# A Strassen-like product for one more K tile pair of the MLP's second matrix, with its blocks in another order

## The chip, the cores and the metric

The kernel runs on one NeuronCore of a Trainium2 chip. Five engines matter here: TensorE (PE in the profile, and PEld for its weight loads), VectorE (DVE), ScalarE (ACT), GpSimd (POOL, nearly unused here) and SyncE (SP, which issues nearly all of the DMA transfers). Matrices lie in the on-chip memory with 128 partitions; results of TensorE go to PSUM, which has 8 banks of 128 x 512 float32, and are carried off by DVE and ACT. The metric is the device time of one execution in microseconds (us).

## The reference

The reference is a trunk of two decoder layers over 256 positions of width 2048, in float32. What it computes, cut to its core:

```python
for layer in range(2):
    mix = short_conv_mixer(h, ...) if layer == 0 else mla_mixer(h, ...)   # conv, then attention
    h = layer_norm(ALPHA * h + mix, ...)
    h = layer_norm(ALPHA * h + sq_relu_mlp(h, w1[layer], w2[layer]), ...)

def sq_relu_mlp(x, w1, w2):        # x 256 x 2048, w1 2048 x 8192, w2 8192 x 2048
    return jnp.square(jax.nn.relu(x @ w1)) @ w2
```

The change touches the MLP of both layers, and the first load of the kernel.

## The kernel before

Every float32 matrix is used as two parts, a high part (a cast to a reduced float32 format that TensorE multiplies at full pace) and a low part (what the cast left out). ACT makes the high part (L122), DVE the low part (L123); the helper is `split`. A product then takes three passes of TensorE, high by high, high by low and low by high. In `dot` (L284 to L286) each of the three is one matmul of 512 columns. In `products` (W1) the low part of the activations lies beside the high part, so the three passes are one matmul of 512 columns (`high`, L200) and one of 256 (`low`, L204): a pair per K tile.

The weights come through one ordered list, `stream`. Its items are taken in that order by `take`, which on the way loads and splits items that lie ahead, up to `LOOK` = 5 units. A plain item is 128 x 1024 numbers (512 KB), one load on SP, one split, one unit. A fast item is two loads, and counts three units: `prepare` (L143 to L166) makes from its two arrays the seven right-hand factors of a Strassen-like product, with three splits of 1024 columns, one of 512 (`t4`) and three subtractions on DVE (L155, L158, L161). Split parts lie in `whl` (8 buffers each for high and low), loaded arrays in `raws` (5 buffers). The program order is that of the Python text; each engine's own queue is ordered by a planner of the framework, which may move work that is ready ahead of work that is not.

The MLP (`mlp`, L565) works through the 8192 hidden features in eight quarters q of 1024 features ("quarter" is this document's word; there are eight of them, `NQ`). In each, W1 makes eight tiles of 128 hidden features (`products`, eight tiles of 16 pairs; q = 0 goes another way, L661 to L679), and `hidden` carries each tile off: ACT copies half of the PSUM tile, DVE adds the halves (L341), ACT takes relu and square, two tiles at a time are split into `h`, and `form` makes the left-hand factors S1 to S4 of the fast product. Then W2 takes the quarter's eight K tiles into the output of 256 x 2048, which is held in `acc` as two token halves t by four blocks n of 512 columns.

In the quarters `FAST` (q = 1 to 6), blocks 0 and 1 go by `first_pair` (L601): for each of the four pairs j of K tiles, the 2 x 2 block product (two token halves by two K tiles by two column blocks) is done with seven products in place of eight (`fast_products`, L328), into seven PSUM banks. Three of the seven sums are carried into `acc`, the four others into `sums` (`keep`, L593 to L599); `fold` (L610) adds those into `acc` in six DVE instructions during q = 7. Blocks 2 and 3 follow as plain products (`down`, L296): per block, four items of two K tiles, each item with two token halves, two K tiles and three matmuls. The W1 tiles of the quarters use PSUM banks 0 and 1 in turn (L682). In layer 2 the residual is turned by TensorE transposes in the quarters 1 to 4, between block 2 and block 3 (`extra`, `turn_residual`, L953).

At the start, the first four K tiles come each as one array of 768 columns, 256 of the input and 512 of weights (`lead`, L512 to L516). The second of them is issued by ACT, the others by SP.

Of the kernel before, what the change touches and what calls it, by code (L numbers as in the profile page):

```python
# [10 lines left out]
F32 = mybir.dt.float32  # L11
# [5 lines left out]
P = 128  # L17
W = 256 + 2
T = 256
D = 2048  # L20
NC = D // P
FF = 4 * D
NQ = 8
# [11 lines left out]
NB = 4  # L35
BW = D // NB
FAST = range(1, NQ - 1)
FIRST = (0, 1, 2, 3, 4, 6, 8, 12, 16)
LEAD = 4
HEAD = 4  # L40
# [11 lines left out]
def trunk(ctx: ExitStack, tc: tile.TileContext, xT, vecs, lead, w_first, w_in, w_out, w_kv, w_q, w_uk, w_uv,  # L52
# [28 lines left out]
    def mlp_stream(l):  # L81
        out = []
        for q in range(NQ):
            out += halves(w1[l, q * QC:(q + 1) * QC])
            plain = halves(w2[l, q, 2:] if q in FAST else w2[l, q])
            fast = [(w2f[l, q, j, 0], w2f[l, q, j, 1]) for j in range(QC // 2)] if q in FAST else []
            at = 0 if q or q not in FAST else len(plain) // 2
            out += plain[:at] + fast + plain[at:]
        return out

    stream += mlp_stream(0) + halves(w_kv) + halves(w_q)
# [181 lines left out]
    def products(n, x, turned=None, banks=(None,)):  # L273

        for i in range(n):
            w = take()
            ps = psum("ps_u", banks[i % len(banks)])
            mm_run([(w, ps)], x, 0, NC, NC, turned=None if i else turned)
            yield ps


    def dot(ps, w, x, first, last):

        nc.tensor.matmul(ps, x[0], w[0], start=first, stop=False)  # L284
# [37 lines left out]
    OWN, KEPT = ("1", "5", "7", "6"), (2, 3, 4, 5, 6, 7, 0)  # L322
# [5 lines left out]
    def fast_products(ps, x, forms, j, n):  # L328

        b, = take(1)  # L330
        a = {"11": held(x[2 * j], 0), "12": held(x[2 * j + 1], 0), "22": held(x[2 * j + 1], 1)}
        for i in range(4):
            a[f"S{i + 1}"] = [forms[:, j, o, i * P:(i + 1) * P] for o in range(2)]
        for p, l, r in FACTORS:
            dot(ps[p], b[r], a[l], j == 0, j == n - 1)

    def whole(ps, out):

# [173 lines left out]
    for k0, k1 in pieces:  # L512
        if k0 < LEAD:
            r = raws.tile([P, 1024], F32, tag="raw", name=f"lead{k0}")
            (nc.sync if k0 != 1 else nc.scalar).dma_start(r[:, :T + HEAD * P], lead[k0])
# [49 lines left out]
    def mlp(idx, ln, blocks, fast, begin=None, extra=None):  # L565
# [14 lines left out]
        def block(n, t):  # L580
            return acc[:, t, n * BW:(n + 1) * BW]
# [11 lines left out]
        def keep(p, ps):  # L593

            at = sums[:, OWN.index(p)] if p in OWN else block(*{"2": (0, 0), "3": (1, 0), "4": (0, 1)}[p])
            if q == 0 or q == FAST[0] and p in OWN:
                nc.scalar.copy(at, ps)
            else:
                nc.vector.tensor_tensor(at, at, ps, ALU.add)  # L599

        def first_pair(h, forms, banks):  # L601

            n = QC // 2
            ps = {p: psum(f"ps_f{p}", bank) for (p, _, _), bank in zip(FACTORS, banks)}
            for j in range(n):
                fast_products(ps, h, forms, j, n)
            for p in ps:
                keep(p, ps[p])

        def fold():  # L610

            s1, s5, s7, s6 = (sums[:, i] for i in range(4))
            both = acc[:, 1, :2 * BW].rearrange("p (b c) -> p b c", b=2)
            right = acc[:, :, BW:2 * BW]
            two = lambda v: v.unsqueeze(1).to_broadcast([P, 2, BW])
            for d, a, b in ((block(0, 0), block(0, 0), s1), (s6, s6, s1), (block(1, 0), block(1, 0), s6),
                            (s7, s7, s6), (both, both, two(s7)), (right, right, two(s5))):
                nc.vector.tensor_tensor(d, a, b, ALU.add)
                yield

        for q in range(NQ):
            ht = act.tile([P, QC, 2 * T], F32R, tag="c", name=f"h{idx}_{q}")
            h = [ht[:, k, :] for k in range(QC)]
# [80 lines left out]

# [409 lines left out]
```

## Time and profile before

| | us |
|---|---|
| median of 3 runs | 2025.61 (2025.37 to 2025.71) |
| the profiled execution | 2025.47 |
| its span, first to last instruction | 2023.7 |
| PE busy / PEld busy | 2016.2 / 1762.2 |
| DVE busy / ACT busy | 1606.0 / 1175.8 |
| HBM read | 381.78 MB, 190 GB/s over the span |
| one quarter q = 2 (540.22 to 625.45) | 85.23 |
| of it W1, blocks 0 and 1, blocks 2 and 3 | 44.39, 19.08, 21.76 |

The profile's group rows read: line of the kernel, engine, operation, tiles written and read, shape and count, busy time and mean duration of one, idle time of the engine before it and what ended that. The mean of a matmul is longer than the step from one matmul to the next, because matmuls are pipelined; steps are read from start times, or from a stretch and a count. In the answers by stretch, each engine's column is its busy time and, in brackets, its instructions.

### The profile page before, as it was taken

Reading aid. Unit: us, or ns where it says so; the run is one execution under the profiler, and the core shown is the slowest. Engines: PE = TensorE matmul, PEld = TensorE weight load, DVE = VectorE, ACT = ScalarE, POOL = GpSimd, SP = SyncE. Lnnn points to the kernel's source line nnn. Section 1 sums busy time; section 2 is a strip of 40 time slices with the busy share of each in tenths; the row PEclk is TensorE's granted clock in tenths of the full one; section 3 lists DMA queues with packets and bytes.
Section 4 is the critical chain, followed back from the end, with each engine's and each line's share of the span. In section 5 each row is a group of like instructions: output and inputs, shape, how many; then the busy total and the mean of one; then the engine's idle time right before and its main releaser. Section 6 shows DMA issues by size and latency. Waiting matters only on the chain.

```text
span 2023.7 us, 30065 instructions
## 1 busy us (share of the span) xinstructions
PE 2016.2 (100%) x11240; PEld 1762.2 (87%) x11240; DVE 1606.0 (79%) x2472; ACT 1175.8 (58%) x1802; POOL 2.3 (0%) x21
## 2 busy tenths in 40 slices
PE   9999999999999999999999999999999999999998
PEld 8888888988888888888889998898888888888886
DVE  7667677788797987879688978776879798797966
ACT  6444445676565665656556655567656556565651
POOL 0000000000000000000000000000000000000000
PEclk9999999999999999999999999999999999999999
DMA  9666666564756657466754544656475664746663
GB/s 320 203 188 189 189 189 186 174 197 140 255 152 214 210 165 248 146 231 200 216 176 151 181 129 136 191 177 197 137 246 168 203 224 144 248 155 211 220 203 119
DMA packets 106705, 385.83 MB, mean 191 GB/s; under 512 B 11840, under 2 KB 12480, under 8 KB 106304
## 3 DMA queue, kind: packets, MB, share of 16 engines
q1 hardware_dynamic: 106416, 383.53, 60.5%
q8 instruction: 88, 1.44, 0.3%
q14 instruction: 57, 0.47, 0.1%
q10 hardware_dynamic: 144, 0.39, 0.1%
HBM read 381.78 MB, written 2.10 MB: 190 GB/s over the span
## 4 chain that ended last, share of the span: by engine, by line
PE 99%; DMA 0%; DVE 0%; ACT 0%; issue 0%; DVEq 0%
PE ps_u L200 20%; PE ps_l L200 13%; PE ps_u L204 11%; PE ps_d L284 7%; PE ps_d L286 7%; PE ps_d L285 7%; PE ps_l L204 7%; PE ps_f L285 4%; PE ps_f L286 4%; PE ps_f L284 4%; PE ps_w L234 2%; PE ps_w L232 2%; PE ps_w L233 2%; PE ps_g L232 1%; PE ps_g L234 1%; PE ps_g L233 1%
## 5 line engine op out<-in xcount | busy, mean ns | idle before, releaser
L123 DVE TENSOR_TENSOR lo<-raw,hi 128x1024 fp32r<-128x1024 f32 x710 | 860.2, 1222 | 314.3 <-ACT hi L122 243.3
L122 ACT CAST hi<-raw 128x1024 fp32r<-128x1024 f32 x710 | 742.3, 1050 | 461.9 <-PE ps_u L200 105.6
L200 PE MATMUL ps_u<-xhl,hi 128*128 128x512 f32 x1792 | 621.0, 392 | 0.0
L204 PE MATMUL ps_u<-xhl,lo 128*128 128x256 f32 x1792 | 499.7, 280 | 0.0
L200 PEld LDWEIGHTS ps_u<-xhl,hi 128*128 128x128 f32 x1792 | 334.5, 187 | 72.1
L204 PEld LDWEIGHTS ps_u<-xhl,lo 128*128 128x128 f32 x1792 | 339.2, 189 | 1.8
L284 PE MATMUL ps_d<-hi,h 128*128 128x512 f32 x640 | 250.0, 391 | 0.0
L286 PE MATMUL ps_d<-hi,h 128*128 128x512 f32 x640 | 249.3, 390 | 0.0
L285 PE MATMUL ps_d<-lo,h 128*128 128x512 f32 x640 | 249.2, 389 | 0.0
L200 PE MATMUL ps_l<-xhl_a,hi 128*128 128x512 f32 x704 | 243.5, 393 | 0.0
L204 PE MATMUL ps_l<-xhl_a,lo 128*128 128x256 f32 x704 | 195.1, 279 | 0.0
L200 PEld LDWEIGHTS ps_l<-xhl_a,hi 128*128 128x128 f32 x704 | 131.9, 188 | 29.4
L286 PEld LDWEIGHTS ps_d<-hi,h 128*128 128x128 f32 x640 | 120.2, 188 | 25.0
L284 PEld LDWEIGHTS ps_d<-hi,h 128*128 128x128 f32 x640 | 120.2, 188 | 24.8 <-DVE fh L341 0.3
L285 PEld LDWEIGHTS ps_d<-lo,h 128*128 128x128 f32 x640 | 120.2, 188 | 24.7
L204 PEld LDWEIGHTS ps_l<-xhl_a,lo 128*128 128x128 f32 x704 | 132.3, 189 | 0.2
L200 PE MATMUL ps_l<-z,hi 128*128 128x512 f32 x240 | 83.9, 399 | 0.0
L652 ACT ACTIVATE fp<-fp 128x256 f32<-128x256 f32 x96 | 40.0, 417 | 74.5 <-DVE fp L341 73.7
L122 ACT CAST hi_t<-raw_t 128x1024 fp32r<-128x1024 f32 x48 | 50.4, 1049 | 41.7 <-DVE raw_t L155 33.4
L234 PE MATMUL ps_w<-xd,hi 128*128 128x258 f32 x256 | 73.0, 285 | 0.0
L232 PE MATMUL ps_w<-xd,hi 128*128 128x258 f32 x256 | 72.6, 284 | 0.0
L233 PE MATMUL ps_w<-xd,lo 128*128 128x258 f32 x256 | 72.5, 283 | 0.0
(261 smaller groups left out, 3134.1 us busy)
## 6 DMA issues: line engine op xcount, KB each, us to landing
raw<-in_w_dram SPq DMA_DIRECT2D x416, 512.0 KB, 4.4
raw<-in_w2f_dram SPq DMA_DIRECT2D x96, 512.0 KB, 3.7
raw<-in_w_in_dram SPq DMA_DIRECT2D x88, 512.0 KB, 3.7
raw<-in_w_out_dram SPq DMA_DIRECT2D x32, 512.0 KB, 3.6
raw<-in_w_o_dram SPq DMA_DIRECT2D x32, 512.0 KB, 3.9
raw<-in_w_kv_dram SPq DMA_DIRECT2D x10, 512.0 KB, 4.3
raw<-in_w_q_dram SPq DMA_DIRECT2D x8, 512.0 KB, 4.4
raw<-in_w_uk_dram SPq DMA_DIRECT2D x8, 512.0 KB, 4.5
```

Of the source, the lines that this page charges most:

```text
L122: nc.scalar.copy(hi, src)
L123: nc.vector.tensor_tensor(lo, src, hi.bitcast(F32), ALU.subtract)
L200: nc.tensor.matmul(ps, w[blk // 8][0][:, blk % 8, :], x, start=first, stop=False)
L204: nc.tensor.matmul(ps[:, :T], w[blk // 8][1][:, blk % 8, :], x[:, :T], start=False, stop=last)
L232: nc.tensor.matmul(ps[:, :W], hi, x[k][:, :W], start=k == 0, stop=False)
L233: nc.tensor.matmul(ps[:, :W], lo, x[k][:, :W], start=False, stop=False)
L234: nc.tensor.matmul(ps[:, :W], hi, x[k][:, W:], start=False, stop=k == NC - 1)
L284: nc.tensor.matmul(ps, x[0], w[0], start=first, stop=False)
L285: nc.tensor.matmul(ps, x[0], w[1], start=False, stop=False)
L286: nc.tensor.matmul(ps, x[1], w[0], start=False, stop=last)
L652: nc.scalar.activation(f, f, AF.Relu)
```

## The change

- **Order of blocks.** In the quarters 1 to 6, blocks 2 and 3 come first and blocks 0 and 1 after them. `down_pairs` replaces `first_pair` and the two calls of `down`, and goes pair by pair over the K tiles.
- **One more fast pair.** `MIXED = "pspp"`: of the four pairs of K tiles of blocks 2 and 3, the second ("s") goes by the seven products too. Products 2, 3 and 4 of it, and the part "22", add into the same four PSUM banks as the plain products of the other pairs; the other four (`OWN`) have banks of their own and are carried into `sums` right after, which is twice as large now. Each quarter thus ends with 15 adds out of PSUM in place of 11, and `fold` has eight instructions of 1024 columns.
- **One matmul in two.** `EVEN`: in the last K tile of one bank, the second of the three matmuls of `dot` is issued as two of 256 columns each, so that a quarter's W2 has an even number of matmuls.
- **Banks.** W1's tiles use four PSUM banks in turn; which four rotates from quarter to quarter (`busy`, `free`). The transposes of `extra` come before the last pair of K tiles.
- **Order of arrays.** The large arrays are laid out in another order and without the small gaps between them; the scratch kept for DMA descriptors shrinks from 4096 to 512 bytes per partition.
- **First K tile.** Its input part is issued by ACT and its weight part by SP; the second K tile moves to SP.

```diff
+MIXED = "pspp"
+EVEN = (QC - 1, "22")
...
-    for tag, columns in (("c", 4096), ("pad0", 64), ("b", 8256), ("a1", 4128), ("pad1", 96), ("a2", 4128), ("pad2", 96)):
+    for tag, columns in (("c", 4096), ("a2", 4128), ("a1", 4128), ("b", 8256)):
...
-            plain = halves(w2[l, q, 2:] if q in FAST else w2[l, q])
-            fast = [(w2f[l, q, j, 0], w2f[l, q, j, 1]) for j in range(QC // 2)] if q in FAST else []
...
+            for j, kind in enumerate(MIXED):
+                out += [(w2f[l, q, 1, j, 0], w2f[l, q, 1, j, 1])] if kind == "s" else \
+                    halves(w2[l, q, 3, j]) + halves(w2[l, q, 2, j])
+            out += [(w2f[l, q, 0, j, 0], w2f[l, q, 0, j, 1]) for j in range(QC // 2)]
...
-    def dot(ps, w, x, first, last):
+    def dot(ps, w, x, first, last, two=False):
         nc.tensor.matmul(ps, x[0], w[0], start=first, stop=False)
-        nc.tensor.matmul(ps, x[0], w[1], start=False, stop=False)
+        for at in (slice(0, T), slice(T, 2 * T)) if two else (slice(None),):
+            nc.tensor.matmul(ps[:, at], x[0], w[1][:, at], start=False, stop=False)
         nc.tensor.matmul(ps, x[1], w[0], start=False, stop=last)
...
-            (nc.sync if k0 != 1 else nc.scalar).dma_start(r[:, :T + HEAD * P], lead[k0])
+            for queue, at in ((nc.scalar, slice(0, T)), (nc.sync, slice(T, T + HEAD * P))) if k0 == 0 else \
+                    ((nc.sync, slice(0, T + HEAD * P)),):
+                queue.dma_start(r[:, at], lead[k0][:, at])
...
-        sums = fast.tile([P, 4, BW], F32, name=f"sums{idx}")
+        sums = fast.tile([P, 4, 2, BW], F32, name=f"sums{idx}")
...
+        def down_pairs(h, forms, busy, free):
+            ps = {p: psum("ps_d", bank) for p, bank in zip(("22", "3", "2", "4"), free)}
+            for j, kind in enumerate(MIXED):
+                if kind == "s":
+                    first, last = j == MIXED.index("s"), j == MIXED.rindex("s")
+                    if first:
+                        ps.update({p: psum(f"ps_f{p}", bank) for p, bank in zip(OWN, busy)})
+                    fast_products(ps, h, forms, j, OWN if first else (), OWN if last else ())
+                    if last:
+                        for p in OWN:
+                            keep(p, 1, ps[p])
+                    continue
+                if extra and q <= NB and j == len(MIXED) - 1:
+                    for t in range(2):
+                        extra(block, q - 1, t, busy[2 + t])
+                for nb, two in ((3, ((1, "22"), (0, "3"))), (2, ((0, "2"), (1, "4")))):
+                    w, = take(1)
+                    for t, p in two:
+                        for kk in range(2):
+                            k = 2 * j + kk
+                            dot(ps[p], wide_rows(w, kk), held(h[k], t), k == 0, k == QC - 1, (k, p) == EVEN)
+                    if j == len(MIXED) - 1:
+                        for _, p in two:
+                            keep(p, 1, ps[p])
             n = QC // 2
+            banks = (*busy, *free)
             ps = {p: psum(f"ps_f{p}", bank) for (p, _, _), bank in zip(FACTORS, banks)}
             for j in range(n):
-                fast_products(ps, h, forms, j, n)
+                fast_products(ps, h, forms, j, ps if j == 0 else (), ps if j == n - 1 else ())
             for p in ps:
-                keep(p, ps[p])
+                keep(p, 0, ps[p])
+            return (banks[7], *banks[:3]), banks[3:7]
...
+        busy, free = (0, 1, 2, 3), (4, 5, 6, 7)
...
-                for m, ps in enumerate(products(QC, xhl, TURNED, (0, 1))):
+                for m, ps in enumerate(products(QC, xhl, TURNED, busy)):
...
-                first_pair(h, forms, KEPT)
-                for n, banks in ((2, (1, 2)), (3, (3, 4))):
-                    down(h, put, n, banks)
-                    if extra and n == 2 and q <= NB:
-                        for t in range(2):
-                            extra(block, q - 1, t, 5 + t)
+                busy, free = down_pairs(h, forms, busy, free)
...
-    nc = _bacc.Bacc("TRN2", target_bir_lowering=False, num_devices=1, dynamic_dma_scratch_size=4096)
+    nc = _bacc.Bacc("TRN2", target_bir_lowering=False, num_devices=1, dynamic_dma_scratch_size=512)
```

More of the change, by code (lines that the diff above doesn't have):

```diff
@@ L84, in mlp_stream @@
             out += halves(w1[l, q * QC:(q + 1) * QC])
-            plain = halves(w2[l, q, 2:] if q in FAST else w2[l, q])
-            fast = [(w2f[l, q, j, 0], w2f[l, q, j, 1]) for j in range(QC // 2)] if q in FAST else []
-            at = 0 if q or q not in FAST else len(plain) // 2
-            out += plain[:at] + fast + plain[at:]
+            if q not in FAST:
+                out += halves(w2[l, q])
+                continue
[3 more added lines that the diff above has]
+            out += [(w2f[l, q, 0, j, 0], w2f[l, q, 0, j, 1]) for j in range(QC // 2)]
         return out
@@ L320, in down_late, with fast_products @@
                 put(n, t, ps)
-    OWN, KEPT = ("1", "5", "7", "6"), (2, 3, 4, 5, 6, 7, 0)
+    OWN = ("1", "5", "7", "6")
     FACTORS = (("3", "S4", "22"), ("1", "11", "11"), ("5", "S1", "T1"), ("7", "S3", "T3"),
                ("2", "12", "21"), ("6", "S2", "T2"), ("4", "22", "T4"))
-    def fast_products(ps, x, forms, j, n):
+    def fast_products(ps, x, forms, j, fresh, ready):
         b, = take(1)
@@ L334, in fast_products @@
         for p, l, r in FACTORS:
-            dot(ps[p], b[r], a[l], j == 0, j == n - 1)
+            dot(ps[p], b[r], a[l], p in fresh, p in ready)
     def whole(ps, out):
@@ L589, in put, with keep @@
                 nc.vector.tensor_tensor(block(n, t), block(n, t), ps, ALU.add)
-        sums = fast.tile([P, 4, BW], F32, name=f"sums{idx}")
-        def keep(p, ps):
-            at = sums[:, OWN.index(p)] if p in OWN else block(*{"2": (0, 0), "3": (1, 0), "4": (0, 1)}[p])
-            if q == 0 or q == FAST[0] and p in OWN:
+        sums = fast.tile([P, 4, 2, BW], F32, name=f"sums{idx}")
+        def keep(p, g, ps):
+            at = sums[:, OWN.index(p), g, :] if p in OWN else \
+                block(*{"2": (2 * g, 0), "3": (2 * g + 1, 0), "4": (2 * g, 1), "22": (2 * g + 1, 1)}[p])
+            if q == FAST[0] and p in OWN:
                 nc.scalar.copy(at, ps)
@@ L599, in keep @@
                 nc.vector.tensor_tensor(at, at, ps, ALU.add)
-        def first_pair(h, forms, banks):
+        def down_pairs(h, forms, busy, free):
[9 more added lines that the diff above has]
+                            keep(p, 1, ps[p])
+                    continue
+                if extra and q <= NB and j == len(MIXED) - 1:
[10 more added lines that the diff above has]
+                            keep(p, 1, ps[p])
@@ L603, in first_pair @@
             n = QC // 2
+            banks = (*busy, *free)
             ps = {p: psum(f"ps_f{p}", bank) for (p, _, _), bank in zip(FACTORS, banks)}
             for j in range(n):
-                fast_products(ps, h, forms, j, n)
+                fast_products(ps, h, forms, j, ps if j == 0 else (), ps if j == n - 1 else ())
             for p in ps:
-                keep(p, ps[p])
+                keep(p, 0, ps[p])
+            return (banks[7], *banks[:3]), banks[3:7]
         def fold():
             s1, s5, s7, s6 = (sums[:, i] for i in range(4))
-            both = acc[:, 1, :2 * BW].rearrange("p (b c) -> p b c", b=2)
@@ L614, in fold @@
[L614 to L617, printed above, removed]
+            c = acc.rearrange("p t (g b c) -> p t b g c", g=2, b=2)
+            for d, a, b in ((c[:, 0, 0], c[:, 0, 0], s1), (s6, s6, s1), (c[:, 0, 1], c[:, 0, 1], s6), (s7, s7, s6),
+                            (c[:, 1, 0], c[:, 1, 0], s7), (c[:, 1, 1], c[:, 1, 1], s7),
+                            (c[:, 0, 1], c[:, 0, 1], s5), (c[:, 1, 1], c[:, 1, 1], s5)):
@@ L1093 @@
         "w2": np.stack([np.stack([_rows(q) for q in w.reshape(NQ, QC * P, D)]) for w in a["mlp_w2"]]),
-        "w2f": np.stack([np.stack([_pairs(q[:, :2 * BW]) for q in w.reshape(NQ, QC * P, D)]) for w in a["mlp_w2"]]),
+        "w2f": np.stack([np.stack([np.stack([_pairs(q[:, 2 * g * BW:2 * (g + 1) * BW]) for g in range(2)])
+                                   for q in w.reshape(NQ, QC * P, D)]) for w in a["mlp_w2"]]),
         "cosT": np.tile(cos, (4, 1)),
```

## The prediction

> **What bounds the kernel now.** I read the page's totals first, then the chain of work that ended last, then the sums by stretch of one quarter.
>
> ```profile
> span 2023.7 us, 30065 instructions
> PE 2016.2 (100%) x11240; PEld 1762.2 (87%) x11240; DVE 1606.0 (79%) x2472; ACT 1175.8 (58%) x1802; POOL 2.3 (0%) x21
> ...
> PE 99%; DMA 0%; DVE 0%; ACT 0%; issue 0%; DVEq 0%
> ```
>
> The chain is TensorE for 99%: PE waits for nobody, so a matmul saved is time saved, as long as everyone else keeps up. How near the others are shows quarter q = 2, by stretch (W1; blocks 0 and 1; blocks 2 and 3; all of it):
>
> ```profile
> 540.22:584.61 44.39, 44.39 (x257) 39.14 (x256) 34.45 (x52) 27.13 (x45) 0.00 (x0) 1.00 0.51 149
> 584.61:603.69 19.08, 19.08 (x86) 15.78 (x85) 18.13 (x25) 11.28 (x16) 0.00 (x0) 1.00 0.53 157
> 603.69:625.45 21.76, 21.76 (x97) 18.02 (x96) 19.07 (x21) 12.64 (x12) 0.00 (x0) 1.00 0.88 312
> 540.22:625.45 85.23, 85.23 (x437) 72.95 (x436) 71.65 (x96) 51.05 (x72) 0.00 (x0) 1.00 0.61 192
> ```
>
> PE is busy throughout at full clock (the 1.00). DVE works 71.65 of 85.23 us (84%), ACT 51.05; so DVE is who could take over.
>
> **TensorE's side.** A plain pair of K tiles of two blocks is 2 blocks x 2 halves x 2 K tiles x 3 = 24 matmuls, the seven products 7 x 3 = 21. A step is read from starts, here from plain matmuls of 512 columns:
>
> ```profile
> 699.81 0.39 PE L284 MATMUL ps_d<-hi,h 128*128 128x512 f32 x1
> ...
> 703.89 0.39 PE L284 MATMUL ps_d<-hi,h 128*128 128x512 f32 x1
> ```
>
> 18 steps in 4.08 us: 226.7 ns. The 84 fast matmuls take 19.08 us, 227.1 ns each. Removed: 24 x 226.7 = 5.44 us; added: 21 x 227.1 = 4.77; so 0.67 us less per quarter. The matmul in two shows nowhere in W2; the nearest is W1's turned order, where two matmuls of 256 columns follow each other:
>
> ```profile
> 455.56 0.40 PE L204 MATMUL ps_u<-xhl,lo 128*128 128x256 f32 x2
> 455.80 0.63 PE L200 MATMUL ps_u<-xhl,hi 128*128 128x512 f32 x2
> 456.27 0.28 PE L204 MATMUL ps_u<-xhl,lo 128*128 128x256 f32 x1
> ```
>
> The two take 0.24 us (one whole: 0.227), and the two behind them 0.47 (0.453): it costs 0.03 us, between 0.01 and 0.05. Left: 0.64 us per quarter, in 6 quarters of 2 layers: **12 x 0.64 = 7.7 us less**. The transposes of layer 2 only change place within W2: 0.
>
> **DVE's side of the same edit.** The rows of that quarter, 540.22 to 625.45:
>
> ```profile
> L123 DVE TENSOR_TENSOR lo<-raw,hi 128x1024 fp32r<-128x1024 f32 x32 | 38.6, 1222 | 12.3 <-ACT hi L122 12.2
> L123 DVE TENSOR_TENSOR lo_t<-raw_t,hi_t 128x1024 fp32r<-128x1024 f32 x4 | 4.9, 1221 | 0.1
> L155 DVE TENSOR_TENSOR raw_t<-raw,raw 128x1024 f32<-128x1024 f32 x4 | 4.9, 1220 | 1.0 <-issue 1.0
> ...
> L161 DVE TENSOR_TENSOR raw<-raw 128x512 f32<-128x512 f32 x4 | 2.8, 689 | 0.1
> ...
> L123 DVE TENSOR_TENSOR t<-raw,t 128x512 fp32r<-128x512 f32 x4 | 2.7, 684 | 0.0
> L158 DVE TENSOR_TENSOR raw<-raw,raw_t 128x512 f32<-128x512 f32 x4 | 2.7, 684 | 0.0
> L599 DVE TENSOR_TENSOR sums<-sums,ps_f 128x512 f32<-128x512 f32 x4 | 2.6, 682 | 0.0
> ```
>
> A fast item: 4 x 1.22 + 3 x 0.69 = 6.95 us; the two plain items it replaces 2.44; four more adds out of PSUM 2.73. Together 7.2 more, but neighbours overlap: back to back the 1024-column forms step by 1.13 and the others by 0.60,
>
> ```profile
> 574.29 2.35 DVE L123 TENSOR_TENSOR lo<-raw,hi 128x1024 fp32r<-128x1024 f32 x2
> 576.56 0.42 DVE L341 TENSOR_TENSOR fp<-ps_u,t 128x256 f32<-128x256 f32 x1
> ...
> 609.50 0.68 DVE L599 TENSOR_TENSOR sums<-sums,ps_f 128x512 f32<-128x512 f32 x1
> 610.10 0.68 DVE L599 TENSOR_TENSOR acc<-acc,ps_f 128x512 f32<-128x512 f32 x1
> ```
>
> (2.27 us from 574.29 to 576.56 for two; 0.60 from 609.50 to 610.10), so 6.32 - 2.27 + 2.40 = 6.5 us more: DVE 78.1 of a quarter of 84.6, **92%**. Room on average, 6.5 us; what matters is the densest stretch, W2. `whl`'s 8 buffers let at most 8 units be ready ahead. When W1 ends (call it 0) these can be: first pair 2, fast pair 3, third pair 2, one of the fourth. From there to the end of W2 PE takes 16.3 + 24 us: 3 x 5.44 + 5 x 4.77 = 40.2. In that time DVE must do: one or two items of the fourth pair (2.3), four fast items (4 x 6.32 = 25.3), eight adds that must leave banks (4.8), the last two W1 tiles' carrying off, `h` and factors (0.34 + 0.60 + 0.60 + 4 x 0.20 = 2.3), and W1's next two units (2.3): **37.0 of 40.2 us**. In layer 2's quarters 1 to 4 two turned adds make it 38.2. The slack is 3.2 and 2.0 us. Can DVE run that full? Around the start of the fast products it does:
>
> ```profile
> 573.51:584.61 11.10, 11.10 (x66) 9.79 (x65) 10.96 (x18) 7.35 (x14) 0.00 (x0) 1.00 0.51 152
> 584.61:594.14 9.53, 9.53 (x44) 7.90 (x43) 9.53 (x16) 5.72 (x10) 0.00 (x0) 1.00 0.39 110
> ```
>
> 20.5 of 20.6 us. From those rows I take PE's wait as 0; the ends are 0 and, if DVE loses as much as it did idle in the fast stretch (0.95 of 19.08, so 2.0 of 40.2 us), still 0, but with nothing left in layer 2. Beyond that each lost us is a us of PE. Who is queued behind a late DVE: the splits of the third and fourth fast item, then W1's first units of the next quarter. The perfect planner's order is the assumption here (rival 2).
>
> The other waits. The adds of the fast pair's four own products free `busy` banks 5.4 us before the transposes want two of them; plain sums "22" and "3" are complete 2.7 us before the last fast products begin, and those want the banks as fifth and sixth product, 2.7 us in: 0. W1 with four banks in place of two: the matmuls of W1 had 0.0 us idle before them, so 0.
>
> ```profile
> L200 PE MATMUL ps_u<-xhl,hi 128*128 128x512 f32 x1792 | 621.0, 392 | 0.0
> L204 PE MATMUL ps_u<-xhl,lo 128*128 128x256 f32 x1792 | 499.7, 280 | 0.0
> ```
>
> ACT gains 1.05 + 0.62 us per quarter, hidden (34 us free). SP issues as many 512 KB loads as before (two plain less, two fast more). `fold` grows from 4 x 0.60 + 2 x 1.13 to 8 x 1.13 us, 4.4 us more during W1 of q = 7, where DVE is busy 27.39 of 44.39 us: 0, and if that cover were gone 4.4 x 2.
>
> ```profile
> 966.39:1010.78 44.39, 44.39 (x258) 39.14 (x256) 27.39 (x34) 25.90 (x44) 0.53 (x1) 1.00 0.70 212
> ```
>
> **The order of arrays and the even count.** W1's pairs do not always go at one pace. In the quarter they take 44.39 / 128 = 346.8 ns. The conv output's product, from the same array tag "b", goes slower, by the chain in order of time:
>
> ```profile
> 281.11 0.47 PE ps_l L200 x2
> ...
> 362.48 0.96 PE ps_l L204 x8
> ```
>
> Between 281.58 and 362.48 lie 229 pairs: 353.3 ns, 6.5 more, with no wait shown. Same array, two paces: the base address alone does not set it, but how a stage is entered may. In all 12 fast quarters W1 went at 346.8, each entered after an even number of matmuls; the split keeps that (94 + 84 = 178). I take 0. Ends: all W1 pairs slow, 1792 x 6.5 = +11.6 us; the conv output's 256 pairs fast, -1.7.
>
> **The first K tile.**
>
> ```profile
> 0.73 0.41 ACTq L515 DMA_DIRECT2D lead<-in_lead_dram  x1
> 0.74 1.33 SPq L515 DMA_DIRECT2D lead<-in_lead_dram  x3
> ...
> 5.12 0.40 ACT L525 CAST xhl_a<-lead 128x256 fp32r<-128x256 f32 x1 [2.67 <-DMA lead<-in_lead_dram]
> ...
> 5.78 0.39 PEld L193 LDWEIGHTS ps_g<-xhl_a,hi 128*128 128x128 f32 x2 [1.06 <-ACT hi L122]
> ```
>
> The first tile lands at 5.1, sharing the engines with the second, which will now queue behind it; the cast of the input can also start before the weights land. Even larger loads land sooner after issue in the steady state:
>
> ```profile
> raw<-in_w_in_dram SPq DMA_DIRECT2D x88, 512.0 KB, 3.7
> ```
>
> 3.7 against 4.36 us bounds the landing's gain at 0.7, and the earlier cast at 0.4 more. Loss: SP issues one load more ahead of the rest, 0.44 us (1.33 / 3), if the later tiles were what PE waits for. I take **0.4 less**, ends +0.4 and -1.1.
>
> **The sum**, against the profiled execution's 2025.47 (its span and 1.8 us around it): 2025.47 - 7.7 - 0.4 = 2017.4. The median is 0.14 higher: **2017.5 us**, 0.4% faster.
>
> **The rivals.**
> 1. *W1 loses its pace* (the even count or the addresses do not hold it): 2017.5 + 11.6 = **2029.1**, no measurable change. For: two paces exist. Against: 12 of 12 stages entered alike.
> 2. *DVE becomes the bound in W2.* If its queue is ordered so that it stands at the four adds of the fast pair until that pair ends (10.2 us) before it starts the last four fast items, it still owes 2.4 + 25.3 + 2.4 + 2.3 = 32.4 us and ends at 42.6, when W1's first unit was due at 40.2 and the fast items' last factor at 39.5: PE waits about 1.2 us, 2.4 where the turned adds come too. 8 x 1.2 + 4 x 2.4 = 19.2: **2036.7**, slower. It decides from a loss of about 3.2 + 0.7 us of DVE in the stretch. For: 92%. Against: today's planner puts ready splits ahead, DVE idle 0.1 us around the fast products.
>
>    By the Trainium skill (Perfetto Trace Analysis, Identifying the Most-Contended Engine) DVE's occupancy is a fair measure of its load, while TensorE's is to be judged by its weight loads' share. By that rule the trace's 87% for PEld leave TensorE room, and DVE at 92% is the engine to relieve: it speaks for this rival and its 2036.7. The trace agrees on the shares, yet PE's chain of 99% says that its steps are gapless.
> 3. *The arrays' order mends the conv output's pace*: **2015.8**.
>
> **How the numbers follow.** As forecast 0.58 (own range 2016.5 to 2020), rival 3 0.06, rival 1 0.14, rival 2 0.22. What a measurement of this kernel can tell from no change is 0.2%, 4.05 us. Faster: 0.58 + 0.06 = 0.64; same: 0.14; slower: 0.22. The range reaches from 2014.5 (rival 3 with the first tile's -1.1) over rival 1 into rival 2, to 2033, which leaves out most of rival 2.
>
> **What would show it.** PE x11216 (12 x 2 fewer); 24 more loads of fast items; a quarter of 84.6 us; W1 still 44.39; PE's first weight load near 5.4; DVE near 78 us a quarter. Wrong it is if W1 takes 45.2 (rival 1), or if PE's rows show idle time ended by DVE's splits at the last fast items or W1's first tile (rival 2).

## The result, and the profile after

The changed kernel takes 2038.53 us (median of 4 runs, 2037.62 to 2041.14), the kernel before 2025.51 in the same comparison: 1.0066 times as long, 95% interval 1.0053 to 1.0079. It is slower by 13 us, where 8 us less was forecast. The profiled execution of the changed kernel took 2039.21 us.

The page's totals of the changed kernel, and its chain of work that ended last:

```profile
span 2037.4 us, 30058 instructions
PE 2016.3 (99%) x11216; PEld 1754.6 (86%) x11216; DVE 1686.7 (83%) x2576; ACT 1191.3 (58%) x1834; POOL 2.3 (0%) x21
...
PE 74%; DVE 18%; DMA 3%; issue 3%; ACT 1%; DVEq 0%; ACTq 0%
```

TensorE has its 24 matmuls fewer, yet the chain, which was TensorE for 99%, now goes through DVE for 18% of the span. Here is quarter q = 3 by stretch: W1; W2's first plain pair and six of the seven products of the fast pair; the seventh and the last two plain pairs; the last four fast pairs; all of it.

```profile
624.72:669.11 44.39, 44.39 (x257) 39.12 (x256) 37.83 (x55) 30.00 (x46) 0.00 (x0) 1.00 0.73 246
669.11:678.67 9.56, 9.56 (x44) 7.89 (x43) 6.68 (x10) 5.03 (x9) 0.00 (x0) 1.00 0.43 133
678.67:690.27 11.60, 11.60 (x54) 9.62 (x52) 11.53 (x17) 5.80 (x8) 0.00 (x0) 1.00 0.31 90
690.27:712.49 22.22, 20.20 (x86) 15.50 (x84) 22.05 (x26) 11.45 (x13) 0.00 (x0) 1.00 0.53 163
624.72:712.49 87.77, 85.75 (x436) 72.13 (x434) 78.09 (x105) 52.29 (x74) 0.00 (x0) 1.00 0.59 192
```

W1 is unchanged at 44.39. W2 takes 9.56 + 11.60 + 22.22 = 43.4 us, where it took 40.84 before. DVE's 78.09 us of work are what was forecast (78.1). But it is full only in the last 34 us (11.53 of 11.60, 22.05 of 22.22) and idles in the stretch before (6.68 of 9.56): 2.9 us lost at the one place, and TensorE waits at the other. TensorE's waits in the changed kernel (what waited and for what: us in total, times, longest), then DVE's waits for the arrays of fast items, in the changed kernel and in the one before:

```profile
PE ps_f L291 <- DVE lo_t L128: 11.8, 15, 1.0
PE ps_f L289 <- ACT hi_t L127: 1.7, 7, 0.3
...
PE ps_f L289 <- DVE acc L608: 0.9, 3, 0.4
```

```profile
DVE raw_t L160 <- DMA raw<-in_w2f_dram: 52.2, 24, 4.1
```

```profile
DVE raw_t L155 <- DMA raw<-in_w2f_dram: 3.0, 6, 1.2
```

DVE stood 3.0 us at such loads before and 52.2 us now, 4.4 per quarter. In quarter 3 it looks like this, by DVE's timeline:

```profile
670.94 1.21 DVE L128 TENSOR_TENSOR lo<-raw,hi 128x1024 fp32r<-128x1024 f32 x1
672.07 0.28 DVE L676 TENSOR_TENSOR sf<-fp 128x128 f32<-128x128 f32 x1
674.40 1.23 DVE L160 TENSOR_TENSOR raw_t<-raw,raw 128x1024 f32<-128x1024 f32 x1 [2.05 <-DMA raw<-in_w2f_dram]
```

The subtraction at 674.40 begins the first of the last four fast items, 5.3 us after W1's end. Why its load came late shows SP, which issues the loads. First its waits from 666 to 677 us that a split of DVE ended, then the issue of that item's second array; then the same issue with seven load buffers (a run of the experiments below):

```profile
SPq L138 <- DVE lo L128: 3.8, 2, 2.2
```

```profile
670.11 0.33 SPq L138 DMA_DIRECT2D raw<-in_w2f_dram  x1
```

```profile
662.81 0.33 SPq L138 DMA_DIRECT2D raw<-in_w2f_dram  x1
```

The two waits end at the item's two issues, 667.52 and 670.11, each within 0.03 us of the end of a split that gave its load buffer back; the second array landed 4.2 us after its issue, and DVE stood until then. With seven buffers the same array is issued 4.9 us before W1's end, here 1.0 us after it.

In the kernel before, the four `raw_t` of quarter 3 begin at 23.6, 11.9 and 2.0 us before W1's end and 7.6 us after it; now the last of five begins 36.2 us after it. Some 34 us behind DVE's stand TensorE pays, by its timeline:

```profile
707.03 0.39 PE L292 MATMUL ps_f<-hi,h 128*128 128x512 f32 x1
707.67 0.49 PE L289 MATMUL ps_f<-hi_t,forms 128*128 128x512 f32 x1 [0.26 <-ACT hi_t L127]
709.18 0.50 PE L291 MATMUL ps_f<-lo_t,forms 128*128 128x512 f32 x1 [1.01 <-DVE lo_t L128]
```

The step is 0.227 us; from 707.67 to 709.18 it is 1.51. Waits like these come at the T1 product of the fourth of the last fast items in ten of the twelve quarters, and of the third too in five. The other two quarters, the first of each layer (q = 1), had none, though DVE stood at loads for 1.8 and 2.2 us early in their W2 too: there ACT, not DVE, carries the eight `OWN` sums (`keep`), and DVE had 36.2 and 37.3 us to do.

Over the 12 quarters W2 takes 508.8 us (40.20 to 43.96 each; the four with turned adds hold 0.89 us of transposes). Without a wait it would be 12 x 40.20 + 4 x 0.89 = 486.0, so the waits cost 22.9 us; before, W2 took 12 x 40.84 + 3.6 = 493.6. The account of the two profiled executions: W2 +15.2, the conv output's product -1.6, the input's two stretches +0.6, the opening -0.1 (these three below), the rest of the span -0.4: 13.7 us, from 2025.47 to 2039.21.

### The profile page after: what moved, and what is told of

Its sections match the earlier page's. It is cut to its first block, busy times and chain, and to the rows that moved or that the text cites. A ratio compares the mean times of both kernels' runs of the same rounds, so it can differ in the third digit from the quotient of the medians.

```text
span 2037.4 us, 30058 instructions
## 1 busy us (share of the span) xinstructions
PE 2016.3 (99%) x11216; PEld 1754.6 (86%) x11216; DVE 1686.7 (83%) x2576; ACT 1191.3 (58%) x1834; POOL 2.3 (0%) x21
## 4 chain that ended last, share of the span: by engine, by line
PE 74%; DVE 18%; DMA 3%; issue 3%; ACT 1%; DVEq 0%; ACTq 0%
PE ps_u L205 15%; PE ps_l L205 13%; PE ps_u L209 8%; PE ps_l L209 7%; DVE lo L128 6%; PE ps_d L291 4%; PE ps_d L292 4%; PE ps_d L289 4%; DMA raw<-in_w2f_dram 2%; DVE lo_t L128 2%; DVE raw_t L160 2%; PE ps_w L239 2%; PE ps_w L237 2%; PE ps_w L238 2%; PE ps_f L291 1%
## 5 line engine op out<-in xcount | busy, mean ns | idle before, releaser
L128 DVE TENSOR_TENSOR lo<-raw,hi 128x1024 fp32r<-128x1024 f32 x710 | 861.3, 1221 | 189.7 <-ACT hi L127 121.1
L127 ACT CAST hi<-raw 128x1024 fp32r<-128x1024 f32 x710 | 739.1, 1049 | 297.6 <-PE ps_l L205 95.7
L289 PE MATMUL ps_d<-hi,h 128*128 128x512 f32 x556 | 217.2, 391 | 0.0
L292 PE MATMUL ps_d<-hi,h 128*128 128x512 f32 x556 | 216.8, 390 | 0.0
L291 PE MATMUL ps_d<-lo,h 128*128 128x512 f32 (+1 forms) x568 | 216.7, 385 | 0.0
L291 PEld LDWEIGHTS ps_d<-lo,h 128*128 128x128 f32 x568 | 106.7, 188 | 21.7
L292 PEld LDWEIGHTS ps_d<-hi,h 128*128 128x128 f32 x556 | 104.4, 188 | 21.5
L289 PEld LDWEIGHTS ps_d<-hi,h 128*128 128x128 f32 x556 | 104.5, 188 | 21.2
L127 ACT CAST hi_t<-raw_t 128x1024 fp32r<-128x1024 f32 x60 | 63.1, 1052 | 93.9 <-DVE raw_t L160 93.9
L160 DVE TENSOR_TENSOR raw_t<-raw,raw 128x1024 f32<-128x1024 f32 x60 | 73.3, 1221 | 52.2 <-DMA raw<-in_w2f_dram 52.2
L127 ACT CAST t<-raw 128x512 fp32r<-128x512 f32 x60 | 37.1, 619 | 70.2 <-DVE raw L166 70.2
L128 DVE TENSOR_TENSOR lo_t<-raw_t,hi_t 128x1024 fp32r<-128x1024 f32 x60 | 73.1, 1219 | 1.5 <-ACT hi_t L127 1.5
```

Of the source, the lines that this page charges most:

```text
L127: nc.scalar.copy(hi, src)
L128: nc.vector.tensor_tensor(lo, src, hi.bitcast(F32), ALU.subtract)
L160: nc.vector.tensor_tensor(t.rearrange(two, a=2), b12.unsqueeze(1).to_broadcast([P, 2, BW]), r1.rearrange(two, a=2), ALU.subtract)
L291: nc.tensor.matmul(ps[:, at], x[0], w[1][:, at], start=False, stop=False)
```

## The experiments

The theories. **Loads**: five load buffers (`raws`) hold back the fast items. A fast item takes two for its arrays and a third for `raw_t`, and an array of a fast item landed 4.1 us after its issue (median; 3.7 before), so DVE stands and comes late into a W2 that needs all of its time. **Work alone**: DVE has 6.5 us more to do per quarter, and W2 has no room for that, whatever the loads do. Beside them, where the small differences come from: the array order, the even count and the first K tile.

### All of the change but the fast pair

```diff
-MIXED = "pspp"
-EVEN = (QC - 1, "22")
+MIXED = "pppp"
+EVEN = None
-            s1, s5, s7, s6 = (sums[:, i] for i in range(4))
+            s1, s5, s7, s6 = (sums[:, i, :1] for i in range(4))
```

(The output `c` of `fold` is narrowed in the same way.)

> The changed kernel with its one fast pair taken back: the four pairs of blocks 2 and 3 are all plain, no matmul is split (96 + 84 are even already), fold covers blocks 0 and 1 alone. All else of the change stays: order of blocks, banks, arrays, first K tile. Both theories (DVE has too much work in W2; loads come too late for the last four fast items): PE waits nowhere in W2, the fast stretch of a quarter is back at 19.05 us. The 22.9 us of waits of the changed kernel go, 12 x 0.64 = 7.7 us of matmuls come back: 2038.5 - 22.9 + 7.7 = 2023.3 us, that is 2.2 under the kernel before. If instead the order of blocks or the banks are what makes PE wait, waits stay and it is above 2028.

Measured: 2024.42 us (10 runs, 2023.97 to 2024.91), 0.9994 times before, interval 0.9985 to 1.0004. TensorE has no wait in W2, which is 40.84 us in every quarter. A quarter, W1 and W2, by stretch:

```profile
624.00:668.39 44.39, 44.39 (x258) 39.12 (x256) 34.79 (x51) 28.86 (x45) 0.00 (x0) 1.00 0.71 226
668.39:709.23 40.84, 40.84 (x182) 33.80 (x181) 36.94 (x46) 23.27 (x27) 0.00 (x0) 1.00 0.53 167
```

So the order of blocks, the four banks and the moved transposes cost W2 nothing: the loss belongs to the fast pair. The time is 1.1 us over the 2023.3 expected. DVE works 71.73 us here against 78.09.

### Two subtractions left out

The changed kernel without the subtractions of L163 and L166; factors T2 and T4 are then not what the product needs.

```diff
-        nc.vector.tensor_tensor(b12, b22, t[:, :BW], ALU.subtract)
-        nc.vector.tensor_tensor(t4, b21, b12, ALU.subtract)
```

> The changed kernel without two of the three subtractions of each fast item (the two of 512 columns); the output is no longer the reference's. Loads, splits, buffers, matmuls stay. Theory A (DVE's work in W2 is more than fits): 10 x 0.60 = 6.0 us less DVE per quarter, more than the 1.9 us that PE waits per quarter on average, so the waits go to under 2 us in all: 2016 to 2018 us. Theory B (the second array of the last four fast items is loaded too late, since the five load buffers are held): DVE still stands about 50 us in all at those loads and PE still waits at least half of its 22.9: above 2027.

Measured: 2016.33 us (4 runs), 0.9955, interval 0.9940 to 0.9969. W2 is 40.20 in every plain quarter. Quarter 3 by stretch, and DVE's waits at loads:

```profile
623.20:667.59 44.39, 44.39 (x257) 39.12 (x256) 37.29 (x53) 29.67 (x47) 0.00 (x0) 1.00 0.70 230
667.59:707.79 40.20, 40.20 (x181) 33.28 (x179) 35.06 (x42) 21.74 (x28) 0.00 (x0) 1.00 0.52 156
```

```profile
DVE raw_t L160 <- DMA raw<-in_w2f_dram: 22.4, 27, 1.9
```

With 5.7 us less work per quarter (72.35 in place of 78.09) nothing waits, though DVE still stands 22.4 us at loads and the first of the last four fast items still begins 2.7 us after W1's end. It shows that late loads alone do not cost TensorE anything. The time is where theory A (work) had it, and of theory B (loads) both numbers missed, the 50 us of stand and the time above 2027. It does not separate the theories by itself: without the two instructions the buffers also come free sooner, and the stand itself fell from 52.2 to 22.4 us.

### Four, six and seven load buffers

Three edits that change no work, only the number of buffers. With six, the second buffer of T4 is given up for room, or one of the eight split buffers; with seven, one split buffer.

```diff
-RAW, WA = 5, 8
+RAW, WA = 6, 8
-        f = state["fast"].tile([P, 2, BW], F32R, tag="t4", name=f"t4_{i}", bufs=2)
+        f = state["fast"].tile([P, 2, BW], F32R, tag="t4", name=f"t4_{i}", bufs=1)
```

> The changed kernel with six load buffers in place of five; to find the room, the right-hand factor T4 has one buffer in place of two. Theory A (work): DVE's idle time at the loads of fast items falls from 52 us in all, but its work in W2 stays at about 40 us in 40, so PE's waits fall by less than half: above 2028. Theory B (loads): DVE starts the last four fast items 2 to 4 us earlier, which is as much as PE waits: 2016 to 2020. If one buffer for T4 binds, the row that writes T4 shows idle time ended by PE, and the time is above 2038.

```diff
-RAW, WA = 5, 8
+RAW, WA = 6, 7
```

> The changed kernel with six load buffers in place of five and seven split buffers in place of eight; T4 keeps its two buffers. If what the sixth load buffer gave was the earlier start of the last four fast items, and the waits that were left with it came from the single T4 buffer (2.6 us of PE's waits by its rows), then the fast stretches are at 19.05 us but for the quarters with turned adds: 2015.5 to 2018. If the eight split buffers are what lets DVE run ahead, as the prediction had it, seven cost more than the sixth load buffer gives: above 2025.

```diff
-RAW, WA = 5, 8
+RAW, WA = 7, 7
```

> As the run before, with seven load buffers. Theory B (loads): DVE no longer stands at the loads of fast items (52 us in the changed kernel, under 10 here), and no quarter has a PE wait: 2015.5 to 2016.5. Theory A (work alone): no better than with six.

```diff
-RAW, WA = 5, 8
+RAW, WA = 4, 8
```

> The changed kernel with four load buffers (`raws`) in place of five; the same instructions on every engine. Load buffers decide: a fast item holds three of them through DVE's chain, so with four the second array of the next one can't be under way; from six to five buffers the time above the floor in the last four fast pairs went from 5.3 to 22.9 us, so with four it grows by at least as much again: 2055 to 2080 us, with TensorE's waits in every quarter of W2 and the first of the last four fast items started later than 2 to 5 us after W1's end. Rival, only the amount of DVE's work in W2 counts: that amount is the same, so 2038.5 us stays within 3.

Measured (load buffers, split buffers, T4 buffers; the waits are the sum of W2 above 486.0 in the profiled execution; DVE's stand is its wait at `raw_t`; its idle time is that in the twelve W2, by stretch):

| buffers | time us | to before, 95% interval | W2's waits us | DVE's stand at loads us | DVE idle in W2 us |
|---|---|---|---|---|---|
| 4, 8, 2 | 2056.75 | 1.0154 (1.0133 to 1.0175) | 38.3 | 44.7 | 50.5 |
| 5, 8, 2 (the change) | 2038.53 | 1.0066 (1.0053 to 1.0079) | 22.9 | 52.2 | 36.7 |
| 6, 8, 1 | 2021.13 | 0.9976 (0.9966 to 0.9985) | 5.3 | 27.7 | 27.3 |
| 6, 7, 2 | 2022.40 | 0.9985 (0.9975 to 0.9994) | 2.2 | 25.8 | 14.6 |
| 7, 7, 2 | 2020.89 | 0.9975 (0.9965 to 0.9986) | 0.8 | 16.5 | 14.3 |

The work of the engines is the same in all five. "Work alone" has no place for the 18 us between five and seven buffers, in which the granted clock of the twelve W2 was 1.00 throughout; it falls. Of the 38.3 us with four buffers some 8 are not waits (an estimate): in five of the twelve W2 the granted clock was at half for 3.4 us, which is 1.7 us each. That time is the median of two runs, 2053.11 and 2060.39. Quarter 3 with seven load buffers, W1 and W2 by stretch, with the sum of both:

```profile
623.30:667.69 44.39, 44.39 (x257) 39.12 (x256) 38.76 (x57) 29.27 (x46) 0.00 (x0) 1.00 0.72 244
667.69:707.89 40.20, 40.20 (x181) 33.28 (x179) 39.30 (x50) 23.66 (x29) 0.00 (x0) 1.00 0.51 153
sum 84.59, PE 84.59 PEld 72.39 DVE 78.06 ACT 52.93 POOL 0.00; mean PE 42.30 PEld 36.20 DVE 39.03 ACT 26.46 POOL 0.00
```

DVE does the same 78.06 us; what differs is that it hardly stands still in W2: 39.30 of 40.20, where the change had DVE idle for 2.9 us early in W2 and TensorE behind for 3.2 us at its end. The first of the last four fast items begins 0.5 us after W1's end, in place of 2 to 5. So both are needed for the loss: a W2 in which DVE has 39 to 40 us to do, and 2 to 4 us of it in which DVE stands idle.

Misses in these runs: with four buffers DVE's stand at `raw_t` is no longer than with five (another row, `DVE lo L128 <- ACT hi L127`, has 152.2 us in place of 123.6, and DVE's idle time in W2 did grow), and two quarters of twelve had no wait at all, where I expected one in each. With six load buffers and one T4 buffer TensorE waited at another place, `PE ps_f L291 <- DVE t L128`, 2.6 us. All three versions with six or seven buffers were slower than theory B had them (2016 to 2020, 2015.5 to 2018, 2015.5 to 2016.5), and with seven the stand was 16.5 us, not under 10. With seven split buffers part of that lies outside the fast quarters, at the kernel's end: TensorE's wait for `udiag` is 3.0 us in place of 1.2, and behind it the six matmuls can run slower. The profiled execution with six load buffers, then that with seven:

```profile
2012.62 4.54 PE L1038 MATMUL offset<-gbt,udiag 128*128 128x512 f32 x6 [2.99 <-DVE udiag L1036]
```

```profile
2011.16 2.84 PE L1038 MATMUL offset<-gbt,udiag 128*128 128x512 f32 x6 [2.99 <-DVE udiag L1036]
```

In the first the granted clock was at half for 3.4 us from 2012.7 on, in the second at full speed during these matmuls. With seven load buffers the six of eight runs with a mean granted clock of 0.999 took 2020.8 to 2021.3 us, the two with 1.000 took 2018.8 and 2020.0. What the split buffers have to do with the end I did not find out. The versions with seven load buffers and with six and eight split buffers are faster than the kernel before by 0.25% and 0.24%; between these two the runs don't decide.

The Trainium skill (Perfetto Trace Analysis, Optimization Strategy) says that the same gap coming back through a stretch can mean too few buffers for the next tile. The traces agree: DVE's stand at `raw_t` came back in each of the 12 quarters, 52.2 us in all with five load buffers and 16.5 with seven. The Trainium skill looks for it on the engine that should be saturated; here it stood on DVE, one engine away from the one that paid.

### Looking further ahead

Seven load buffers, and the stream taken six units ahead.

```diff
-LOOK = 5
-RAW, WA = 5, 8
+LOOK = 6
+RAW, WA = 7, 7
```

> Seven load buffers, seven split buffers, and the stream taken up to six units ahead in place of five. If load buffers were the whole cause, seven have removed it already and looking further ahead gives nothing: 2019 to 2022 us, the same as seven and seven. If what is left above 2017.5 comes from DVE's work being started too late by the program's order, it falls by up to 3 us.

Measured: 2022.21 us (10 runs, 2021.01 to 2024.43), 0.9984, interval 0.9975 to 0.9994: nothing gained on 2020.89. In its profile all quarters' W2 are at the floor of 40.20, or 41.09 with transposes, so the last 0.8 us of waits went; but the stretch between the layers is 1.9 us longer than with `LOOK` = 5 and the end 1.4 us. So the program's order held W2 back by 0.8 us at most once loads had seven buffers.

### The sums of the left-hand factors on GpSimd

A cheaper way to take work off DVE, if it worked: the four instructions of S1 to S4 (128 x 128, 0.28 to 0.29 us each on DVE, 48 of each).

```diff
-                nc.vector.tensor_tensor(s1, a21, a22, ALU.add)
+                nc.gpsimd.tensor_tensor(s1, a21, a22, ALU.add)
```

(and the three below it)

> The changed kernel with the four small instructions that make S1 to S4 moved from DVE to the idle GpSimd; the output is the same. Theory A (work): 16 x 0.20 = 3.2 us less DVE per quarter against 1.9 us of PE's waits on average and 3.2 at most: waits under 5 us in all, 2016 to 2021. Theory B (loads): these instructions lie ahead of the loads' waits and do not free a load buffer earlier: above 2032. If GpSimd and DVE get in each other's way, DVE's instructions grow longer than 1.22 and 0.68 us and the time is above 2038.

Measured: 2090.67 us (4 runs), 1.0321, interval 1.0305 to 1.0336. The groups by shape of this run, then the same `h` split in the changed kernel:

```profile
L676 POOL TENSOR_TENSOR sf<-fp 128x128 f32<-128x128 f32 x48 | 47.5, 989 | 1263.7 <-ACT fp L687 1263.7
L677 POOL TENSOR_TENSOR sf<-sf,fp 128x128 f32<-128x128 f32 x48 | 37.4, 780 | 3.8
L128 DVE TENSOR_TENSOR h<-fp,h 128x512 fp32r<-128x512 f32 x48 | 43.4, 904 | 0.0
```

```profile
L128 DVE TENSOR_TENSOR h<-fp,h 128x512 fp32r<-128x512 f32 x48 | 32.9, 686 | 2.0 <-ACT h L127 1.8
```

On GpSimd one takes 0.77 to 0.99 us on average, and the mean of DVE's split of `h` goes from 686 to 904 ns. By the timeline, 40 of the 48 splits had a GpSimd instruction beside them and took about 0.95 us; the 8 that had none took 0.68. Of the GpSimd instructions, the 37 with no DVE instruction beside them took 0.46 us. DVE's total fell by 14 us (1686.7 to 1672.9), and the time rose by 52. The left-hand factors come later, W2 takes 42.1 to 49.3 us, and TensorE waits for DVE and ACT at several places; which of them costs how much I did not separate. In nine of the twelve W2 the granted clock was at half for 3.4 us. The Trainium skill (Perfetto Trace Analysis, Optimizing Scalar/DVE Operations) warns that moving work between these two might not help, since they share a read port; the 0.95 us beside GpSimd against 0.68 without agree.

### The even count, the order of arrays, the first K tile

Plain pairs only, as in the first experiment, but with the one matmul in two, so that W2 has 181 matmuls:

```diff
-EVEN = None
+EVEN = (QC - 1, "22")
```

> The kernel without the one fast pair, with one matmul of each quarter's W2 in two, so that W2 has 97 + 84 = 181 matmuls, an odd number; PE waits for nobody in it, so the paces are clean. If the evenness holds W1's pace, W1 takes 44.39 us in the quarters entered after an even number and about 45.2 in the others (2, 4, 6 of layer 1), 0.83 more each: about 2024.4 + 5 in all. If not, W1 takes 44.39 throughout and the split costs 0.03 us a quarter: 2024.4 to 2024.9.

Measured: 2024.40 us (one run). W1 takes 44.39 us in all 12 quarters, entered after an odd count too, and W2 40.88 in place of 40.84. The even count sets nothing here; the split costs 0.04 us.

The kernel before with the new order of arrays and the smaller scratch, nothing else:

```diff
-    for tag, columns in (("c", 4096), ("pad0", 64), ("b", 8256), ("a1", 4128), ("pad1", 96), ("a2", 4128), ("pad2", 96)):
+    for tag, columns in (("c", 4096), ("a2", 4128), ("a1", 4128), ("b", 8256)):
...
-    nc = _bacc.Bacc("TRN2", target_bir_lowering=False, num_devices=1, dynamic_dma_scratch_size=4096)
+    nc = _bacc.Bacc("TRN2", target_bir_lowering=False, num_devices=1, dynamic_dma_scratch_size=512)
```

> The kernel before with the new order of the arrays and the smaller descriptor scratch, nothing else. If the arrays' places set the pace of the pairs, the conv output's product takes 83.2 us in place of 84.8, and the input's two stretches 0.3 us more each, as in the changed kernel: 2024.5. If these come from how the stages are entered, the kernel runs as before: 2025.5.

Measured: 2024.44 us (one run), before 2025.53. The conv output's product in the kernel before, then in this run:

```profile
278.49:363.27 84.78, 84.78 (x482) 73.64 (x481) 63.95 (x103) 44.62 (x61) 0.00 (x0) 1.00 0.64 184
```

```profile
279.19:362.40 83.21, 83.21 (x482) 73.36 (x481) 63.20 (x103) 44.70 (x61) 0.00 (x0) 1.00 0.63 188
```

It goes 1.6 us faster, with TensorE busy throughout in both, and the two stretches of the input's products 0.3 us slower each (129.5 and 115.4 in place of 129.2 and 115.1): the same numbers as in the changed kernel. So the order of the arrays and the smaller scratch, which this run does not separate, set these paces: -0.9 us by these three stretches, -1.1 by the time of the one run.

The kernel before with the first K tile from two queues, nothing else:

```diff
-            (nc.sync if k0 != 1 else nc.scalar).dma_start(r[:, :T + HEAD * P], lead[k0])
+            for queue, at in ((nc.scalar, slice(0, T)), (nc.sync, slice(T, T + HEAD * P))) if k0 == 0 else \
+                    ((nc.sync, slice(0, T + HEAD * P)),):
+                queue.dma_start(r[:, at], lead[k0][:, at])
```

> The kernel before with only the first K tile's load changed (input part by ACT's queue, weight part by SP's, the second tile moved to SP). First tile's step as predicted: TensorE's first weight load near 5.34 in place of 5.78, and the end 0.4 us earlier. What the changed kernel's trace suggests: the start 0.44 earlier, but the first product 0.38 longer (22.92 in place of 22.54), as the later tiles land later: the end within 0.1 us of before. If the 0.38 came from the arrays' order instead, the first product here stays 22.54 long.

Measured: 2025.97 us (one run; before 2025.57). The input's first cast, TensorE's first weight load and the casts of the third and the fourth K tile, by the timeline:

```profile
4.28 0.41 ACT L527 CAST xhl_a<-lead 128x256 fp32r<-128x256 f32 x1 [1.82 <-DMA lead<-in_lead_dram]
...
4.93 0.39 PEld L193 LDWEIGHTS ps_g<-xhl_a,hi 128*128 128x128 f32 x2
...
7.32 0.41 ACT L527 CAST xhl_a<-lead 128x256 fp32r<-128x256 f32 x1 [0.73 <-DMA lead<-in_lead_dram]
...
8.86 0.41 ACT L527 CAST xhl_a<-lead 128x256 fp32r<-128x256 f32 x1 [0.33 <-DMA lead<-in_lead_dram]
```

TensorE starts 0.85 us earlier here (4.93; before 5.78; 5.34 in the changed kernel), and the first product is 0.96 us longer (23.51 us; before 22.54; 22.92 in the changed kernel). The next stage begins 0.1 us later than before. The third and the fourth tile land at 7.30 and 8.84 us here, at 6.19 and 7.16 before; their casts now wait for them and come at 7.32 and 8.86, before at 7.34 and 8.45. So the earlier start is waited away at these tiles. My number for the start (5.34) missed, and it is not steady: in the run without the fast pair it was 4.92. That nothing is won held.

## Why the prediction was wrong

The step that failed is the one on DVE's side: "`whl`'s 8 buffers let at most 8 units be ready ahead", from which "37.0 of 40.2 us" followed, and then "From those rows I take PE's wait as 0". The eight split buffers were not the limit: with one fewer and six or seven load buffers nearly all waits go. The five load buffers were.

Two terms of the sum failed with it. The work was 40.3 us in quarter 3, in place of 37.0: four plain splits were still to do at W1's end, where I had one or two (2.3 us more), and two carryings off of W1 tiles and two splits of factors ran in W2, where the sum has one of each (with `h` and the sums about 1.0 us more). And DVE was idle for 3.1 us in it, 2.05 of them at one load and 0.83 at the next split behind that load; I had bounded this by 2.0 from a stretch of the kernel before in which it never stood at a load. The work that ran over took the slack of 3.2 us, and the stand became TensorE's 3.2 us. With less work (two subtractions left out) or less stand (seven load buffers: 39.3 us of work and 0.9 idle) nothing waits in this W2. Load buffers alone, five to seven, move the time from 2038.53 to 2020.89. I had named the fast items' third load buffer nowhere, though `raws` and its 5 buffers stood in the description.

Point by point:

- **TensorE's 7.7 us less: right.** W2 without a wait went from 40.84 to 40.20, the 0.64 forecast, with x11216 matmuls. Where DVE keeps up, the gain is there: with seven load buffers the profiled execution took 2019.96, and the forecast of 2017.5 with the terms since measured (arrays -1.0, the first tile's 0.4 not won, TensorE's longer wait at the end +1.8, one quarter's waits +0.8) is 2019.5. Most runs of that version took another 1 us, with a mean granted clock of 0.999.
- **DVE's 78.1 us per quarter: right** (78.09). 92% on average was no reason for a wait, as the run with seven buffers shows; nor was it safe.
- **Transposes, `fold`, SP: 0, right**, by the run without the fast pair. **Banks: 0 there**, but in the changed kernel the sixth product of the first of the last four fast items waited for an add in three quarters, 0.9 us by the row (`ps_f L289 <- DVE acc L608`): the adds stood in the queue of a late DVE.
- **W1's pace: kept, but not by the even count**, which made no difference. **The order of arrays: taken as 0, was -1.0**; rival 3 was right in its -1.7 for the conv output (-1.6 measured), and I had not seen that the input's stretches would give 0.6 back. The range's lower end of 2014.5 is a slip: its terms give 2015.1.
- **The first K tile: -0.4 forecast, 0 measured.** The start came where I said (near 5.4), but I priced it as if the first load alone set the opening; the third and the fourth took the gain back.
- **Rival 1** did not occur in the changed kernel: 44.39 in every quarter.
- **Rival 2** had the sign and the engine. That its size came out too (2036.7; 2038.5 measured) is luck: it asked for a loss of 3.2 + 0.7 us at the counted work, and 3.1 were lost with 3.3 us more work. Its mechanism was another one: DVE was to stand at the four adds of the fast pair, and it stood at loads. The profile's 87% and 92%, which I set beside it, spoke for it. For its chance of 0.22 I had looked for a loss in the order of DVE's queue alone.

## What to carry to other kernels

When an engine at 92% of the time gets denser work, count for each buffer pool how many items its slots let lie ready when the dense stretch begins, loads as well as results; the pool that runs dry first decides (here the loads), and an item that holds three slots counts three. A stand of 2 to 4 us on a side engine was harmless here while its next stretch had that much room, and turned into waits of TensorE when it had not: check the two together. Before taking such a change back, give the tight pool one or two slots more: here that turned +0.66% into -0.25%.

## What was not expected of the hardware

- The pace of TensorE's pairs (512 and 256 columns) in the conv output's product changed from 84.8 to 83.2 us by the order of the arrays and a smaller scratch alone, without any wait in either profile.
- Short waits of TensorE can be followed by a lower clock. Below is the W2 of quarter 3 with four load buffers, and 3.4 us of it behind two waits of 1.2 and 1.0 us: the granted clock is 0.51 there, and a step is 0.43 us in place of 0.227. It came in five W2 of that run, in nine with the sums on GpSimd, and at the end of two runs behind a wait of 3.0 us, each time for 3.4 us. Other waits of the same size passed without it; what decides stays open.

```profile
672.45:717.88 45.43, 42.90 (x180) 34.14 (x179) 41.32 (x54) 22.52 (x30) 0.00 (x0) 0.96 0.47 150
...
713.60:717.00 3.40, 3.40 (x10) 2.62 (x9) 3.40 (x6) 0.66 (x2) 0.00 (x0) 0.51 0.92 289
```

- W1 can lose its pace behind waits: with four load buffers three of twelve W1 stages took 45.20, 45.48 and 45.93 us (0.5 of the last is a wait) in place of 44.39, and one of 45.22 came with six. In the second row below TensorE is busy throughout and at full clock, as in the first; the quarters ahead of such a stage had waits, but most stages behind waits kept 44.39, all twelve with the sums on GpSimd among them, so what decides stays open. Two W1 stages of the run with four load buffers, by stretch:

```profile
538.86:583.25 44.39, 44.39 (x257) 39.12 (x256) 35.94 (x49) 31.51 (x49) 0.00 (x0) 1.00 0.73 234
...
717.88:763.08 45.20, 45.20 (x257) 39.19 (x256) 39.23 (x55) 32.00 (x49) 0.00 (x0) 1.00 0.73 240
```

- A GpSimd instruction of 128 x 128 with two inputs took 0.46 us with no DVE instruction beside it and 0.77 to 0.99 us on average, against 0.28 to 0.29 on DVE; DVE's split of `h` took about 0.95 us beside one and 0.68 without.
